# Rotating 96 images: the first and last 16 in pieces of 4 with 8-row runs, and the first loads on two queues

## The chip, the cores and the metric

The kernel runs on one core of a Trainium2 chip. The metric is the time of one execution on the device in microseconds (us). Executions of one kernel agree within about 0.3%, so a few tenths of a microsecond need several rounds on the same chip.

## The reference

```python
def setup_inputs():
    batch, c, h, w = 32, 3, 256, 256
    return {"x": np.random.randn(batch, c, h, w).astype(np.float32)}

def reference(x: np.ndarray) -> np.ndarray:
    return np.rot90(x, k=1, axes=(-2, -1)).astype(np.float32)
```

There are 96 images of 256x256 float32, each turned by 90 degrees. 25.17 MB are read and 25.17 MB are written, whatever the method.

## The kernel before

Six groups of 16 images. A group is loaded by two DMAs of 2 MB from the sync queue, turned by 16 VectorE transposes (32x32 blocks, 512 elements per partition each), and stored by two DMAs of 2 MB from the scalar queue. Three input tiles S and three output tiles U rotate. A partition holds 16 rows of one image, so a contiguous run is 16 KB.

```python
    P = 128; R = 16; K = H // R; A = 32 // K; G = 4 * A * A; F = R * W   # joined here on one line
    x_v = x.rearrange("b c h w -> (b c h w)").rearrange(
        "(g b a qk f) -> g b qk a f", b=A, a=A, qk=4 * K, f=F)
    o_v = out.rearrange("b c h w -> (b c h w)").rearrange(
        "(g b a qk f) -> g a qk b f", b=A, a=A, qk=4 * K, f=F)
    in_pool = ctx.enter_context(tc.tile_pool(name="in_pool", bufs=3))
    out_pool = ctx.enter_context(tc.tile_pool(name="out_pool", bufs=3))

    for g in range(N // G):
        S = in_pool.tile([P, A, F], fp32, name="S")
        for b in range(A):
            nc.sync.dma_start(out=S[:, b], in_=x_v[g, b])
        U = out_pool.tile([P, A, F], fp32, name="U")
        src = S.rearrange("p b (r k q) -> p q r k b", r=R, q=R)[:, ::-1, :, ::-1]
        dst = U.rearrange("p a (q k r) -> p q r k a", q=R, r=R)
        for q in range(R):
            nc.vector.transpose(dst[:, q], src[:, q])
        for a in range(A):
            nc.scalar.dma_start(out=o_v[g, a], in_=U[:, a])
```

Every transpose writes a part of both halves of U, so no store of a group can be issued before all 16 transposes are done. And the partitions of a DMA follow the order (qk, a): 64 steps of one stride times 2 of another, where a plain block of 128 rows has one stride.

## Time and profile before

| | before |
|---|---|
| median time | 124.6 us (124.37 to 124.67, 3 runs) |
| span of the profiled execution | 122.7 us |
| VectorE busy | 90.7 us, 74% |
| bytes moved | 50.34 MB, mean 410 GB/s |

The page cuts the span into 40 slices of 3.07 us. Each digit is the busy share of a slice in tenths; the row of GB/s is what the DMA engines moved.

```profile
span 122.7 us, 182 instructions
DVE  0000699999999999999999999999906999930000
DMA  3999999999999999999999999999999999999992
GB/s 85 406 433 443 427 427 427 427 427 427 310 432 432 433 433 427 427 433 432 419 433 438 427 427 427 432 438 432 432 427 438 438 427 433 433 427 427 427 432 101
```

VectorE (DVE) idles in slices; the DMA engines do not. Their rate is flat but for the ends and one dip in slice 10, 31 to 34 us. The view of waits says what VectorE waited for:

```profile
DVE U L49 <- DMA S<-in_x_dram: 13.3, 1, 13.3
DVE U L49 <- DMA out_dram<-U: 4.1, 1, 4.1
```

VectorE's timeline gives its start, 13.33 us, and the end of the last group: 93.14 + 15.20 us, so the last two stores are issued at 108.4 us. The next table of rates (columns: stretch in us, its length, VectorE busy, GpSimd busy, TensorE clock, DMA share, GB/s) gives the dip a size.

```profile
13.33 60.28 DVE L49 STREAM_TRANSPOSE U<-S 128x512 f32<-128x512 f32 x64 [13.33 <-DMA S<-in_x_dram]
93.14 15.20 DVE L49 STREAM_TRANSPOSE U<-S 128x512 f32<-128x512 f32 x16 [4.15 <-DMA out_dram<-U]
```

```profile
1.50:2.00 0.50, 0.00 (x0) 0.00 (x0) 1.00 0.00 0
2.00:3.00 1.00, 0.00 (x0) 0.00 (x0) 1.00 1.03 262
4.00:30.00 26.00, 16.67 (x18) 0.00 (x0) 1.00 1.01 434
30.00:35.00 5.00, 5.00 (x7) 0.00 (x0) 1.00 0.96 351
35.00:90.00 55.00, 53.81 (x58) 0.00 (x0) 1.00 1.01 431
```

Loads alone (4 to 30 us) run as fast as loads and stores together (35 to 90 us). Between 30 and 35 us, 80 GB/s are missing for 5 us, which is 0.9 us of work.

For differences of tenths of a microsecond I add up the trace's packet records and call "lost time" at time t: t minus the bytes moved by then divided by 428.7 GB/s, a reference rate close to that of the flat stretches. It grows where the DMA engines move less than that. All of "lost" below is this sum; the packets themselves run slightly faster than 428.7, so it falls slowly while nothing is wrong. Each figure comes from one profiled execution. A difference of 0.1 or 0.2 us between two profiles says little.

### The profile page before, as it was taken

The page shows a single profiled execution, that of the slowest core. Times are in us where ns is not written, and L with a number is a line of the kernel's source. Part 1 is how long each engine was busy: PE and PEld are TensorE (multiplying, and loading weights), DVE is VectorE, ACT ScalarE, POOL GpSimd, SP SyncE. Part 2 cuts the span into 40 slices and gives each one's busy share as a digit, 9 for nine tenths or more (in the row PEclk, how much of TensorE's full clock was granted, in tenths as well). Part 3 has the DMA queues.
Part 4 walks back from the last instruction along what each step waited for, and adds up shares of the span by engine and source line. Part 5 has one row for each costly group of instructions (what it writes and reads, how often), then busy time and mean ns, then how long its engine had stood idle before and what let it go on. Part 6 is the DMA issues. An engine that isn't in the chain of part 4 may idle for free.

```text
span 122.7 us, 182 instructions
## 1 busy us (share of the span) xinstructions
DVE 90.7 (74%) x96; POOL 0.2 (0%) x4
## 2 busy tenths in 40 slices
DVE  0000699999999999999999999999906999930000
POOL 0000000000000000000000000000000000000000
DMA  3999999999999999999999999999999999999992
GB/s 85 406 433 443 427 427 427 427 427 427 310 432 432 433 433 427 427 433 432 419 433 438 427 427 427 432 438 432 432 427 438 438 427 433 433 427 427 427 432 101
DMA packets 3457, 50.34 MB, mean 410 GB/s; under 512 B 384, under 2 KB 384, under 8 KB 384
## 3 DMA queue, kind: packets, MB, share of 16 engines
q1 hardware_dynamic: 1728, 25.17, 48.9%
q10 hardware_dynamic: 1728, 25.17, 47.9%
q14 instruction: 1, 0.01, 0.0%
HBM read 25.17 MB, written 25.17 MB: 410 GB/s over the span
## 4 chain that ended last, share of the span: by engine, by line
DMA 53%; DVE 31%; SPq 1%; issue 1%; DVEq 1%; ACTq 0%
DVE U L49 31%; DMA out_dram<-U 28%; DMA S<-in_x_dram 26%; SPq L43 1%; DVEq L77 1%; ACTq L51 0%; DVEq L49 0%
## 5 line engine op out<-in xcount | busy, mean ns | idle before, releaser
L49 DVE STREAM_TRANSPOSE U<-S 128x512 f32<-128x512 f32 x96 | 90.7, 1055 | 17.7 <-DMA S<-in_x_dram 13.3
L66 POOL MEMSET const-uint8-127<- 128x1 uint8 x1 | 0.1, 102 | 0.0
L66 POOL MEMSET const-bfloat16-1.0<- 128x1 bf16 x1 | 0.1, 101 | 0.0
L66 POOL MEMSET const-float32-0.0<- 128x1 f32 x1 | 0.1, 98 | 0.2 <-issue 0.2
L66 POOL MEMSET const-float32-1.0<- 128x1 f32 x1 | 0.1, 98 | 0.0
## 6 DMA issues: line engine op xcount, KB each, us to landing
S<-in_x_dram SPq DMA_DIRECT2D x12, 2048.0 KB, 22.3
out_dram<-U ACTq DMA_DIRECT2D x12, 2048.0 KB, 23.3
```

The lines of the kernel that those rows point to most:

```text
L43: nc.sync.dma_start(out=S[:, b], in_=x_v[g, b])
L49: nc.vector.transpose(dst[:, q], src[:, q])
L66: nc = _bacc.Bacc("TRN2", target_bir_lowering=False, num_devices=1)
L77: with _tile.TileContext(nc) as tc:
```

## The change

Its intent: let VectorE and the stores start after 1 MB instead of 4 MB, let the last stores follow the last loads piece by piece, and keep the 16-row form in between. A piece is 4 images: 128 plain runs of 8 KB, one transpose of 2048 elements per partition, one store of 1 MB. The loads of the first four pieces alternate between the sync and the scalar queue.

```diff
+    KINDS = [1, 2, 2, 2, 2, 1]
-    for g in range(N // G):
+    for g, kind in enumerate(KINDS):
...
+        if kind == 1:
+            R = 8
+            Sv = S.rearrange("p (s f) -> p s f", s=4)
+            Uv = U.rearrange("p (s f) -> p s f", s=4)
+            xv = xf[g].rearrange("(s p f) -> s p f", s=4, p=P)
+            ov = of[g].rearrange("(s p f) -> s p f", s=4, p=P)
+            for s in range(4):
+                eng = nc.scalar if g == 0 and s % 2 else nc.sync
+                eng.dma_start(out=Sv[:, s], in_=xv[s])
+            for s in range(4):
+                src = Sv[:, s].rearrange("p (r k q) -> p q r k", r=R, q=R)[:, ::-1, :, ::-1]
+                dst = Uv[:, s].rearrange("p (q k r) -> p q r k", q=R, r=R)
+                nc.vector.transpose(dst, src)
+                nc.scalar.dma_start(out=ov[s], in_=Uv[:, s])
+        else:
...            (the 16-row form as before)
```

More of the change, by code (lines that the diff above doesn't have):

```diff
@@ L20 @@
     P = 128
-    R = 16
-    K = H // R
-    A = 32 // K
-    G = 4 * A * A
-    F = R * W
-    fp32 = mybir.dt.float32
-    x_v = x.rearrange("b c h w -> (b c h w)").rearrange(
-        "(g b a qk f) -> g b qk a f", b=A, a=A, qk=4 * K, f=F
-    )
-    o_v = out.rearrange("b c h w -> (b c h w)").rearrange(
-        "(g b a qk f) -> g a qk b f", b=A, a=A, qk=4 * K, f=F
-    )
+    G = 16
+    KINDS = [1, 2, 2, 2, 2, 1]
+    assert len(KINDS) * G == N
+    F = G * H * W // P
+    fp32 = mybir.dt.float32
@@ L37 @@
+    xf = x.rearrange("b c h w -> (b c h w)").rearrange("(g f) -> g f", g=N // G)
+    of = out.rearrange("b c h w -> (b c h w)").rearrange("(g f) -> g f", g=N // G)
     in_pool = ctx.enter_context(tc.tile_pool(name="in_pool", bufs=3))
     out_pool = ctx.enter_context(tc.tile_pool(name="out_pool", bufs=3))
-    for g in range(N // G):
-        S = in_pool.tile([P, A, F], fp32, name="S")
-        for b in range(A):
-            nc.sync.dma_start(out=S[:, b], in_=x_v[g, b])
-        U = out_pool.tile([P, A, F], fp32, name="U")
-        src = S.rearrange("p b (r k q) -> p q r k b", r=R, q=R)[:, ::-1, :, ::-1]
-        dst = U.rearrange("p a (q k r) -> p q r k a", q=R, r=R)
-        for q in range(R):
-            nc.vector.transpose(dst[:, q], src[:, q])
-        for a in range(A):
-            nc.scalar.dma_start(out=o_v[g, a], in_=U[:, a])
+    for g, kind in enumerate(KINDS):
+        S = in_pool.tile([P, F], fp32, name="S")
+        U = out_pool.tile([P, F], fp32, name="U")
+        if kind == 1:
[13 more added lines that the diff above has]
+        else:
+            R = 16
+            Sv = S.rearrange("p (b f) -> p b f", b=2)
+            Uv = U.rearrange("p (a f) -> p a f", a=2)
+            xv = xf[g].rearrange("(b a qk f) -> b qk a f", b=2, a=2, f=F // 2)
+            ov = of[g].rearrange("(b a qk f) -> a qk b f", b=2, a=2, f=F // 2)
+            for b in range(2):
+                nc.sync.dma_start(out=Sv[:, b], in_=xv[b])
+            src = Sv.rearrange("p b (r k q) -> p q r k b", r=R, q=R)[:, ::-1, :, ::-1]
+            dst = Uv.rearrange("p a (q k r) -> p q r k a", q=R, r=R)
+            for q in range(R):
+                nc.vector.transpose(dst[:, q], src[:, q])
+            for a in range(2):
+                nc.scalar.dma_start(out=ov[a], in_=Uv[:, a])
```

## The prediction

> **What bounds the kernel now.** The DMA engines. The slice rows of the page show DMA at nine tenths in slices 1 to 38 of 40, at 427 to 443 GB/s except 406 in slice 1 and 310 in slice 10. 50.34 MB at about 429 GB/s is 117.4 us of a 122.7 us span. VectorE is busy 90.7 us (74%); the wait view shows two real waits of it, 13.3 us for the first loads and 4.1 us for a store to free a U buffer. Neither leaves the DMA engines idle.
>
> Ledger of the span, from the trace's packet records: first packet at 2.13 us; 0.9 us lost while the first packets ramp (1.1 to 1.5 us each, 0.61 later); 117.4 us of data; 0.75 us lost at 31 to 34 us, where the 12.6 MB of three input buffers are loaded, while the next load and first store, issued at 28.6 us, move nothing before 32 to 33 us; 0.9 us of uneven ends; last packet ends at 121.6, then 1.1 us.
>
> **What the change does.** (1) VectorE starts after 1 MB, not 4 MB. The first two pieces on two queues share the same 16 engines (the Trainium skill, "DMA: Bandwidth & Descriptors", section "Issuing engines are not separate DMA queues": only issue time is saved), so both land at about 8.5 us. Each piece is one transpose of 2048 elements per partition; at before's pitch (16 of 512 in 15.2 us) 3.8 us. Group 0 is done at 23.5 us instead of 28.6; the first store is issued at 12 instead of 28.6. (2) VectorE work stays about 90 us. (3) A third of the bytes move in 8 KB packets instead of 16 KB. The same page, section "Measured", gives about 10.5 ns per packet; before's 16 KB packet takes 611 ns, so I estimate 310 to 315 for 8 KB: 64 extra packets per engine, +0.6 us. No run shows it yet.
>
> **Critical path.** Starting VectorE 5 us earlier is off the critical path: the DMA engines are as busy with loads alone as with both, so earlier stores only displace loads. Group 1 then lands at 26 to 30 us instead of 22, and VectorE idles for it. What can be won is the hole at 31 to 34 us (0.75) and part of the ramp and the end (0.3). I expect no new hole: group 1 is transposed at 42 to 46 us, its successors flow 4 to 5 us later, before the queued 21 MB run dry at 52. At the end finer stores win nothing: before has a backlog of stores from 108 us on.
>
> 124.6 - 0.75 - 0.3 + 0.6, about 124.2 us.
>
> **Prediction: 124.2 us; 123.2 to 125.6 holds it 8 times in 10. Faster by over 2%: 3%; within 2%: 93%; slower by over 2%: 4%.**
>
> **What would show the steps.** Slice 10's dip gone; first transpose at 8 to 9 us, first store at 12 to 13; VectorE busy 88 to 92 us with a new wait of 2 to 8 us for group 1's loads; a 128x2048 transpose of 3.6 to 3.9 us; 415 to 425 GB/s where only 8 KB packets move.
>
> **What would make it wrong.** 8 KB packets of 330 ns or more (+2 us). A new hole near 50 us: up to 1 us. Arbitration by packet starving the last group's loads (8 KB) against stores (16 KB), so that the stores run dry at the end: 1 to 3 us. A slower 128x2048 transpose would hurt only at the end. A gain over 2% would need 122.1 us, less than the DMA floor plus start and end.

## The result and the profile after

The changed kernel took 123.94 us (123.90 to 124.01, 4 runs) against 124.56 us (124.37 to 124.67, 4 runs) for the kernel before: ratio 0.9952, with a 95% interval from 0.9935 to 0.9970. A ratio is the mean time of one kernel's runs over the mean of the other's of the same rounds, so it is not quite the ratio of the medians. The gain is real and is half a per cent; by the 2% rule it counts as "same".

The slices of the page after, VectorE's timeline (start, length, what; in brackets the idle time before it) and its waits:

```profile
span 122.2 us, 172 instructions
DVE  0039999729999999996599993199999999548000
DMA  4999999999999999999999999999999999999993
GB/s 83 418 426 429 445 343 432 464 424 402 426 469 397 429 434 434 429 429 434 429 440 429 429 434 434 424 418 445 418 432 445 402 453 410 464 426 397 426 429 142
```

```profile
8.17 15.44 DVE L50 STREAM_TRANSPOSE U<-S 128x2048 f32<-128x2048 f32 x4 [8.17 <-DMA S<-in_x_dram]
26.77 30.22 DVE L66 STREAM_TRANSPOSE U<-S 128x512 f32<-128x512 f32 x32 [3.16 <-DMA S<-in_x_dram]
...
108.69 3.97 DVE L50 STREAM_TRANSPOSE U<-S 128x2048 f32<-128x2048 f32 x1 [3.15 <-DMA S<-in_x_dram]
```

```profile
DVE U L50 <- DMA S<-in_x_dram: 11.3, 2, 8.2
DVE U L66 <- DMA S<-in_x_dram: 5.5, 2, 3.2
DVE U L66 <- issue: 4.3, 1, 4.3
```

VectorE starts 5.2 us earlier, and then waits 3.16 us for group 1, 3.15 us before the last piece, and elsewhere ("issue" marks a wait whose releaser the profile does not show). Its early start is spent on waits. The dip of slice 10 is gone, but slice 5 has a new one (343 GB/s). The rates by stretch of the changed kernel, for the same places as before:

```profile
1.50:2.00 0.50, 0.00 (x0) 0.00 (x0) 1.00 1.91 262
4.00:14.00 10.00, 5.83 (x2) 0.00 (x0) 1.00 1.03 435
14.00:19.00 5.00, 5.00 (x2) 0.00 (x0) 1.00 0.99 377
19.00:90.00 71.00, 61.16 (x62) 0.00 (x0) 1.00 1.01 430
```

Data now flow before 2 us; in the kernel before they did not. The dip now costs (430 - 377) / 430 x 5 us = 0.6 us instead of 0.9. The lost time tells the same:

| us, from the packet records | before | after |
|---|---|---|
| first packet starts | 2.13 | 1.74 |
| lost at 10 us | 3.00 | 2.70 |
| lost after the dip (at 40; at 20) | 3.70 | 3.22 |
| lost at 110 us | 3.33 | 2.91 |
| last packet ends | 121.59 | 121.06 |

So 0.3 us come from the start and about 0.2 to 0.3 from the dip; the long middle takes a little back (lost time falls more slowly), and the end gives 0.1. The share of the dip is near the scatter of single profiles; what supports it is that the dip was 0.43 to 0.69 us in the four runs that open as the changed kernel does, and 0.79 to 0.94 us in the kernel before, e2 and e5, which open in the old form (e6 is told below).

### The profile page after: what moved, and what is told of

The parts are those of the page before. It is cut to its first block, busy times and chain, and to the rows that moved or that the text cites. A ratio compares the mean times of both kernels' runs of the same rounds, so it can differ in the third digit from the quotient of the medians.

```text
span 122.2 us, 172 instructions
## 1 busy us (share of the span) xinstructions
DVE 91.5 (75%) x72; POOL 0.2 (0%) x4
## 4 chain that ended last, share of the span: by engine, by line
DMA 62%; DVE 27%; SPq 1%; issue 1%; DVEq 0%
DMA S<-in_x_dram 46%; DVE U L66 24%; DMA out_dram<-U 16%; DVE U L50 3%; SPq L45 1%; SPq L61 1%; DVEq L66 0%
## 5 line engine op out<-in xcount | busy, mean ns | idle before, releaser
L66 DVE STREAM_TRANSPOSE U<-S 128x512 f32<-128x512 f32 x64 | 60.6, 1050 | 9.8 <-DMA S<-in_x_dram 5.5
L50 DVE STREAM_TRANSPOSE U<-S 128x2048 f32<-128x2048 f32 x8 | 31.0, 3950 | 11.3 <-DMA S<-in_x_dram 11.3
```

The lines of the kernel that those rows point to most:

```text
L50: nc.vector.transpose(dst, src)
```

## The experiments

Twelve kernels ran, in four batches. The kernel before ran beside each batch, with medians of 124.48 to 124.55 us.

### e1: only the first group in pieces

```diff
-    KINDS = [1, 2, 2, 2, 2, 1]
+    KINDS = [1, 2, 2, 2, 2, 2]
```

> Only the first 16 images in pieces, the last as before. Theory D (the DMA engines bound everything; the change wins about 0.3 us at the start and 0.3 us of the hole at the first store, and pays for half of the 8 KB packets, 0.2 us): 124.1 to 124.3 us, last packet end uneven as before. Rival V (the gain of 0.6 us is VectorE starting 5 us earlier): all of the gain is here, 123.9 us.

Measured: 128.54 us, ratio 1.031 (1.029 to 1.034), correct. Both expectations missed by over 4 us. The slices and VectorE's last groups:

```profile
span 126.2 us, 177 instructions
GB/s 86 418 426 436 447 340 460 426 436 413 439 410 439 434 452 416 421 421 457 436 426 421 421 447 442 431 418 416 442 442 442 421 416 426 405 5 249 478 436 166
```

```profile
78.97 15.20 DVE L66 STREAM_TRANSPOSE U<-S 128x512 f32<-128x512 f32 x16 [4.30 <-issue]
98.37 15.21 DVE L66 STREAM_TRANSPOSE U<-S 128x512 f32<-128x512 f32 x16 [4.20 <-DMA S<-in_x_dram]
```

And from the chain that ended last:

```profile
59.36 38.88 DMA S<-in_x_dram
```

Slice 35 moves 5 GB/s: the DMA engines have nothing to do. The last group starts at 98.37 us, not at 93.14 as before, since its loads have only just landed (the chain of waits ends their DMA at 59.36 + 38.88, about 98.25 us). It finishes at 113.6 us, and no store of it can be issued sooner. The stores queued before it ran dry from about 110.4 us on (their last packet ends at 111.1). Lost time goes from 2.8 us at 110 us to 7.3 at 120: a hole of 4.5 us.

Why did the loads land later, with engines that were never idle until then? Because bytes stored early are bytes not loaded. In the kernel before, all loads had moved by 91.8 us; in e1 by 97.3 us. The earlier stores took that share of the engines. In the kernel before, the spare time at this place was small too: the last stores were issued at 108.4 us, and the packets of the stores ahead of them ended at 111.3. After the dry spell in e1, the first packet came 1.2 us after the issue (113.6 to 114.8), so before had about 1.7 us to spare (111.3 - 108.4 - 1.2), and e1's last group came 5.2 us later.

### e2: only the last group in pieces

```diff
-    KINDS = [1, 2, 2, 2, 2, 1]
+    KINDS = [2, 2, 2, 2, 2, 1]
```

> Only the last 16 images in pieces. Theory D: the hole at 31 to 34 us and the slow start stay as before; finer last stores win about 0.2 us of uneven ends and the 8 KB packets cost 0.2 us: 124.4 to 124.6 us. Rival E (the gain comes from the end, where the last stores can be issued sooner): 123.9 to 124.1 us.

Measured: 124.62 us, ratio 1.0018 (1.0003 to 1.0033). Theory D's figure, just above its range: without the early start, the fine end gains nothing. First packet at 2.13 us, a dip of the old size (lost 2.88 at 30 us, 3.67 at 40), last packet at 121.49.

This run also shows how loads and stores share the engines. From 80 to 90 us the loads of the last group (8 KB packets) moved 1.44 MB and the stores (16 KB packets) 2.86 MB, one to two; in the kernel before, with 16 KB on both, 2.14 and 2.16 MB from 50 to 60 us. The Trainium skill ("DMA: Bandwidth & Descriptors", section "Queues, rings and completion order") says that an engine takes its queues in turn, packet by packet. The trace agrees that they take turns: 176 load packets and 173 store packets started in these 10 us. The turn is smaller here, though: the page calls 9 to 17 descriptors typical of one packet, while here the turns mostly change from one run of 8 or 16 KB to the next (of 95 packets whose successor on the same engine can be told from the times, 75 are followed by one of the other queue). Small packets thus get the smaller share beside large ones, and the last piece of e2 landed only at 102 us.

### e3: all loads on the sync queue

```diff
-                eng = nc.scalar if g == 0 and s % 2 else nc.sync
+                eng = nc.sync
```

> The changed kernel with all loads on the sync queue. Theory D: the first piece lands at about 6 us instead of 8, VectorE and the first store start 2 us earlier, the time moves by no more than 0.2 us (123.8 to 124.1). Rival V (an early VectorE is what pays): faster than the changed kernel by 0.3 us or more. Rival Q (two queues are what pays at the start): slower by 0.3 us or more, 124.2 us and up.

Measured: 123.95 us, ratio 0.9964 (0.9951 to 0.9977), beside 123.94 for the changed kernel in an earlier batch. VectorE started at 5.63 us instead of 8.17, and waited 6.99 us for group 1 instead of 3.16. The two queues pay nothing, and neither does a VectorE that starts 2.5 us sooner. This is what the skill says in "Issuing engines are not separate DMA queues": only issue time is saved.

### e4: all six groups in pieces

```diff
-    KINDS = [1, 2, 2, 2, 2, 1]
+    KINDS = [1, 1, 1, 1, 1, 1]
```

> All six groups in 8-row pieces, so 128 more packets per engine than in the changed kernel. If a pair of 8 KB packets costs 7 ns more than one of 16 KB, as its trace shows (309 against 611 ns): +0.9 us, 124.8 us. At 10.5 ns per packet, as I used in the prediction: +1.3 us, 125.2 us. If the packet cost is hidden: 123.9 us.

Measured: 124.30 us, ratio 0.9989 (0.9977 to 1.0002). It loses about 0.4 us to the changed kernel, where 0.9 and 1.3 were expected. An 8 KB packet is recorded at 309 ns, one of 16 KB at 611; e9 and e10 below give a price from the flat stretch alone. By whole times, e4 against e3 of the same batch is 0.35 us for 128 more pairs of 8 KB packets per engine, 2.7 ns a pair. The forecast of 415 to 425 GB/s for 8 KB packets was missed too: 428 from 20 to 100 us. It has no hole at the end.

### e5: four input buffers, two output buffers

```diff
-    in_pool = ctx.enter_context(tc.tile_pool(name="in_pool", bufs=3))
-    out_pool = ctx.enter_context(tc.tile_pool(name="out_pool", bufs=3))
+    in_pool = ctx.enter_context(tc.tile_pool(name="in_pool", bufs=4))
+    out_pool = ctx.enter_context(tc.tile_pool(name="out_pool", bufs=2))
```

(in the kernel before)

> The kernel before with four input buffers and two output buffers: eight loads are queued at the start, so the loads do not run dry at 31 us, while the first store is still issued at 28.6 us. Theory L (the 0.8 us hole at 31 to 34 us is loads run dry): hole gone, data rate flat at about 429 GB/s from 4 to 40 us. Theory S (the hole is what the first store does to the engines): still 0.5 us or more lost between 31 and 34 us. Both halves: 0.3 to 0.5 us lost. The whole time is not the question here, since two output buffers make VectorE wait later; 124 to 128 us.

Measured: 137.14 us, ratio 1.102, outside the range I gave for the whole time, since VectorE waited 19.0 us for output buffers and the stores ran dry twice at the end. The question was the dip:

```profile
4.00:30.00 26.00, 16.62 (x18) 0.00 (x0) 1.00 1.01 431
30.00:35.00 5.00, 5.00 (x7) 0.00 (x0) 1.00 1.00 347
```

A fourth group of loads was already queued, and the dip is there all the same (347 GB/s; 351 before). The prediction's cause for it, loads run dry, falls. What is left is the first store, issued at about 28.6 us here too.

### e6: the kernel before with its second load on the scalar queue

```diff
-            nc.sync.dma_start(out=S[:, b], in_=x_v[g, b])
+            eng = nc.scalar if g == 0 and b % 2 else nc.sync
+            eng.dma_start(out=S[:, b], in_=x_v[g, b])
```

> The kernel before with the second load of group 0 on the scalar queue, nothing else. If the second queue is what shortens the start: lag at 10 us down from 3.0 to about 2.7, 124.2 to 124.3 us. If the smaller loads are (issued in 0.38 instead of 0.60 us): no change, 124.5 us.

Measured: 124.58 us, ratio 1.0012 (0.9997 to 1.0027). Lost at 10 us: 3.03, as before. The second queue does not shorten the start. But the dip of this profile is much larger: lost time goes from 2.92 us at 30 us to 4.45 at 40, so 1.5 us against 0.8 before. It was the slowest of the six runs (124.89 us), and its next loads and first store were issued at 30.73 us, two microseconds later than before. Whether loads running dry added to this dip, or executions differ that much, no run settles.

### e7, e9 and e10: the DMAs without transposes

Their outputs are wrong, which doesn't matter for the times. e7 is the kernel before without VectorE: each store takes S directly, with six input buffers.

```diff
-    in_pool = ctx.enter_context(tc.tile_pool(name="in_pool", bufs=3))
-    out_pool = ctx.enter_context(tc.tile_pool(name="out_pool", bufs=3))
+    in_pool = ctx.enter_context(tc.tile_pool(name="in_pool", bufs=6))
...            (U, src, dst and the transposes removed)
-            nc.scalar.dma_start(out=o_v[g, a], in_=U[:, a])
+            nc.scalar.dma_start(out=o_v[g, a], in_=S[:, a])
```

> Wrong result on purpose: the loads and stores of the kernel before without transposes, six buffers, each store waits for its load alone. Theory D (DMA bound from first to last packet): 123.5 to 124.5 us, with a loss of about 0.4 us where the first store starts at about 9 us, though loads are queued. Rival V (VectorE's chain matters): 121 us or less.

e9 changes only the order of addresses, to plain blocks of 128 rows; sizes stay at 2 MB and 16 KB runs.

```diff
-        "(g b a qk f) -> g b qk a f", b=A, a=A, qk=4 * K, f=F
+        "(g b p f) -> g b p f", b=A, p=P, f=F
...            (o_v the same)
```

> Wrong result on purpose: the copy (e7) with plain 128x4096 loads and stores, still 16 KB rows and 2 MB, but the partition order of the 8-row pieces. If the simpler order of addresses is what brings the first packet at 1.7 instead of 2.1 us and halves the loss at the first store: first packet at 1.7 us, loss at the first store about 0.5 us, 123.3 to 123.6 us. If the size of rows or of the whole DMA does: as e7, first packet at 2.1 us, loss 1.2 us, 124.2 us.

e10 cuts e9 into 1 MB DMAs of 8 KB runs.

```diff
-        "(g b p f) -> g b p f", b=A, p=P, f=F
+        "(g b p f) -> g b p f", b=4, p=P, f=F // 2
...            (o_v, the tile and the loops accordingly)
```

> Wrong result on purpose: as e9 but in 1 MB pieces with 8 KB rows throughout. If size matters: first packet at 1.7 us and a loss at the first store of about 0.5 us here and not in e9; 4 ns more per pair of 8 KB packets, in all 0.75 us, takes most of it back: 123.9 to 124.3 us.

| | e7 (order as before) | e9 (plain) | e10 (plain, 8 KB) |
|---|---|---|---|
| median time, us | 124.19 | 123.81 | 124.60 |
| ratio to before (95%) | 0.9974 (0.9958 to 0.9990) | 0.9954 (0.9927 to 0.9981) | 1.0004 (0.9981 to 1.0026) |
| first packet, us | 2.12 | 1.74 | 1.73 |
| lost just before the first store's packets (at 10, 10 and 8 us) | 2.97 | 2.83 | 2.79 |
| lost after them, at 20 us | 4.16 | 3.62 | 3.68 |
| lost at 110 us | 3.61 | 3.07 | 3.96 |

Rates by stretch of e7, then of e9:

```profile
1.50:2.00 0.50, 0.00 (x0) 1.00 0.00 0
10.00:15.00 5.00, 0.00 (x0) 1.00 0.96 321
15.00:100.00 85.00, 0.00 (x0) 1.00 1.01 431
```

```profile
1.50:2.00 0.50, 0.00 (x0) 1.00 2.31 426
10.00:15.00 5.00, 0.00 (x0) 1.00 0.98 357
15.00:100.00 85.00, 0.00 (x0) 1.00 1.01 432
```

Four things follow. First, as expected of e7 (123.5 to 124.5 us), the time without any VectorE work is 123.8 to 124.2 us: the changed kernel, at 123.94, is as fast as DMAs alone. Second, the dip is there in e7 with plenty of loads queued, at 10 to 15 us, because there the first store comes early: it goes with the first store. Third, e9 differs from e7 only in the order of addresses, and that alone moves the first packet from 2.12 to 1.74 us and, in these two profiles, makes the dip smaller: lost time at 20 us falls by 0.54 us (4.16 to 3.62), of which 0.40 is the dip (1.19 to 0.79). The size of packets and DMAs does not do that (3.68 in e10). The first packet is firm, since every run with the old order starts at 2.11 to 2.13 us and every run with plain first loads at 1.72 to 1.77. The dip's share is less so: e9's profile is of its fastest run and e7's of its slowest, the medians differ by 0.38 us, and the intervals overlap. Fourth, e10 against e9 prices the small packets: from 20 to 110 us lost time falls by 0.55 us in e9 and rises by 0.28 in e10. 0.83 us over 38.8 MB, or 148 pairs of 8 KB packets per engine, is 5.6 ns a pair. By medians it is 0.79 us for all 192 pairs, 4.1 ns, and e4 gave 2.7. The changed kernel has 64 such pairs per engine: an estimate of 0.17 to 0.36 us.

The expectation of e9 was half right: first packet as in its first theory, dip 0.8 us (3.62 - 2.83) where 0.5 was given. e10's expectation, that size matters, fell: its first packet and its dip are near e9's, and its time, 124.60 us, is above its range. That the dip is 0.5 us in the changed kernel and 0.8 to 0.9 in e9 and e10, all three with a plain first store, stays unexplained.

### e8: a small store at the very start

```diff
+    z_pool = ctx.enter_context(tc.tile_pool(name="z_pool", bufs=1))
+    Z = z_pool.tile([P, 128], fp32, name="Z")
+    nc.vector.memset(Z, 0.0)
+    early = of[0].rearrange("(s p f) -> s p f", s=4, p=P)[3][:, :128]
+    nc.scalar.dma_start(out=early, in_=Z)
```

(in e3, ahead of the loop)

> The one-queue version (e3) with a 64 KB store of zeros at the very start, into bytes that the real store of group 0 overwrites later. If the 0.5 us lost at 13 to 15 us is a one-time price of the first store, it moves into the dead time before 3 us: lag at 20 us about 2.7 instead of 3.16, time 123.5 us. If it is the price of every change from loads alone to loads and stores: lag at 20 us stays near 3.2, time 123.9 to 124.1 us.

Measured: 124.11 us, ratio 0.9973 (0.9953 to 0.9993), correct. Lost at 10 us rose to 2.81 (2.64 in e3), and the later dip shrank (2.81 to 3.14; in e3 2.64 to 3.16). These sums count the early store's own 64 KB as moved; it is extra work, worth 0.15 us more. The price was not moved into dead time: lost at 20 us is 3.14, no better than 3.16, and about what the second theory gave. The dip shrank from 0.52 to 0.33 us, which that theory does not explain, though it is little more than the scatter of profiles. So the first theory's gain did not come, and what makes the price stays open.

### e11 and e12: two tests of e1's hole, both spoiled

```diff
             (e11, in e1: the stores of group 0 after its four transposes)
+            for s in (3, 2, 1, 0):
                 nc.scalar.dma_start(out=ov[s], in_=Uv[:, s])
```

> As e1, but the four stores of group 0 are issued in reverse order, so the first waits for all four transposes: at about 23.8 us instead of 12.3. Theory P (early stores push the loads of the last group back, and the coarse last group then finishes after the stores have run dry): last loads land at 93 to 95 us instead of 98.2, the hole near 110 us shrinks from 4.5 us to 0 to 1.5 us, 124.0 to 125.5 us. Rival (the hole of e1 comes from something else in the pieces, for instance the waits on DMA semaphores): unchanged, 128.5 us.

Measured: 127.99 us, ratio 1.028. The test did not take place: the stores were still issued at 12.17, 15.99, 19.82 and 23.64 us, one after each transpose, so the order written in the source was not the order in which they ran. It is a second run of e1, with the same hole, and says nothing on the theory.

```diff
             (e12, in e1: the last group stores half of each row after 8 transposes)
-            for q in range(R):
-                nc.vector.transpose(dst[:, q], src[:, q])
-            for a in range(2):
-                nc.scalar.dma_start(out=ov[a], in_=Uv[:, a])
+            n = 2 if g == len(KINDS) - 1 else 1
+            for h in range(n):
+                for q in range(h * R // n, (h + 1) * R // n):
+                    nc.vector.transpose(dst[:, q], src[:, q])
+                lo, hi = h * F // 2 // n, (h + 1) * F // 2 // n
+                for a in range(2):
+                    nc.scalar.dma_start(out=ov[a][:, :, lo:hi], in_=Uv[:, a, lo:hi])
```

> As e1, but the last group, still with 16-row runs and coarse loads, stores the first half of each row after 8 of its 16 transposes. Theory P: it lands at 98.2 us as in e1, but stores are issued at 106 and 113.6 us, the queued stores last until about 115 us, so the hole of 4.5 us is gone or under 0.5 us: 123.7 to 124.2 us. Rival (the last group has to be in 8-row pieces because its loads come late): 126 us or more.

Measured: 133.69 us, ratio 1.073, slower than both figures. A line of its waits says why:

```profile
DVE U L68 <- DMA out_dram<-U: 10.4, 1, 10.4
```

The second eight transposes waited for the first half's stores to land, as though they wrote the same bytes. They do not, but the region that one transpose writes spans both halves of the tile, and I take it (argued, not shown) that the tracking of dependencies saw an overlap. Half of the test can be read: with 2.1 MB of stores issued at 106.2 us, the engines stayed busy until about 115.5 us instead of 110.4. With the second half at 113.6 us there would have been almost no hole, but no run shows that.

So e1's cause rests on its own trace, on the comparison with e2 and the changed kernel, and on this half of e12. The test that would change only the moment of group 0's stores is missing, so that the early stores made the loads late is argued from the byte counts (91.8 and 97.3 us), not shown by a run of its own. That pieces in the last group remove the hole is shown (e1 against the changed kernel).

## Why the prediction was right, and where it was not

The time (124.2 predicted, 123.94 measured, range 123.2 to 125.6) was right, and so was its main reason: the DMA engines bound the kernel from the first packet to the last, so VectorE's earlier start is off the critical path. The run without transposes (123.8 to 124.2 us) and e3 show it. Of the details, the first transpose (8.17 us), the first store (12.17), the piece's transpose (15.44 us for four, 3.86 each), and the new waits of VectorE came as said. Four steps did not.

1. "What can be won is the hole at 31 to 34 us (0.75)", because loads run dry. The hole did not go: it moved to 14 to 19 us and shrank to about 0.5 us lost. It goes with the first store, not with dry loads: e5 has loads queued and keeps it, e7 has it early. (e6's larger dip leaves room for dry loads to add to it there.)
2. The start and the end were put at 0.3 us together. The start alone gave 0.3 and the end 0.1. The second queue has no part in it (e3, e6). In the copies, the plain order of addresses is what changes start and dip: 0.54 us less lost by 20 us, from e7 to e9, in one profile each. Before and after differ by 0.53 us at 40 us (3.70 and 3.17). That the same cause acts in the full kernel is likely from this, not shown, since the 8-row form and the plain order come together there.
3. Small packets: +0.6 us predicted from 10.5 ns per packet; the runs give 2.7 to 5.6 ns, an estimate of 0.17 to 0.36 us. The term was sized 1.7 to 3.5 times too large, and it happened to offset the gain that step 1 put too high. That the total came within 0.3 us is in part luck.
4. "At the end finer stores win nothing: before has a backlog of stores from 108 us on." True of the kernel before (e2: 124.62), false of the changed one. The last loads end over 5 us later, since early stores took their share of the engines, and that uses up the backlog. Without pieces in the last group the change costs 4 us (e1: 128.54). I read the worth of the second half from a trace that did not yet have the first half in it.

In numbers: the first half alone +4.0 us, the second alone +0.1 to +0.2, both together -0.6.

No version here clearly beats the changed kernel. e3 has the same time with simpler code.

## What to carry to other kernels

When the DMA engines are busy throughout, as here, an earlier store is a later load: look at which transfer comes last, and whether enough is queued behind it to cover the work between its landing and its store. Two halves of a change have to be judged together, because one may consume the slack on which the other's value was read. And before putting a dip down to an empty queue, run the case in which that queue is full.

## What the Trainium skill lacked or had wrong

- "DMA: Bandwidth & Descriptors", section "Measured": its 10.5 ns per packet is the floor of a 4 KB transfer issued from GpSimd. For the sync and scalar queues here, halving 16 KB packets costs 2.7 (e4 against e3) to 5.6 ns (e9 against e10, flat stretch) for each packet more.
- No page has the price of the first store into a stream of loads: 0.5 to 1.2 us of all 16 engines, once (e7: 1.2; e9: 0.8; changed kernel: 0.5), with loads queued.
- No page says that the order of addresses in a DMA delays its first packet: 64x2 rows of 16 KB started at 2.12 us, 128 plain rows of 16 KB at 1.74 us, both issued at 0.73 us (e7, e9).
- "DMA: Bandwidth & Descriptors", section "Queues, rings and completion order" was right on taking turns, but the turn was mostly one run here and not 9 to 17 descriptors (e2: 75 of 95 packets were followed by the other queue), and it does not draw the conclusion: 8 KB loads beside 16 KB stores got one third of the bandwidth (1.44 against 2.86 MB in 10 us, e2).
